# Two first value projections in one pass over x, and other banks, queues and orders of work at the seams

## The chip, the cores and the metric

The kernel runs on one core of one Trainium2 chip. The metric is the device time of one execution in microseconds. TensorE (PE) multiplies matrices, VectorE (DVE), ScalarE (ACT) and GpSimd (POOL) work on elements, SyncE (SP) issues most of the DMAs. Matmul results stand in PSUM banks, all other data in SBUF.

## What is computed

One transformer layer with native sparse attention (NSA) and a large feed-forward network, a gated embedding, and behind it a second layer with sliding-window attention (SWA) and a convolutional feed-forward network. There are 256 tokens with 2048 features, all in float32. Cut to what matters here:

```python
def first_block(x, ...):
    hn = rms_norm(x, norm_mix)
    q, kc, vc, ks, vs, kw, vw, gates = split(hn @ nsa_w_in)        # 16 heads of 128, 4 groups of keys
    k_cmp = silu(blocks(kc) @ w1_k) @ w2_k                          # and v_cmp: the compression
    o = g0 * att(q, k_cmp, v_cmp) + g1 * att(q, ks, vs) + g2 * att(q, kw, vw)
    h = x + o @ nsa_w_out
    h = h + square(relu(rms_norm(h, norm_ffn) @ ffn_w1)) @ ffn_w2
    h = h + (p @ ple_w_proj) * sigmoid(rms_norm(h, norm_ple) @ ple_w_gate)
    return rms_norm(h, norm_final)

def second_block(x, ...):
    q, k, v = split(rms_norm_2(x, g0) @ swa_w_in)                   # 32 heads of 64, 8 of keys
    x = x + rms_norm_2(softmax_with_sinks(q, k, bias) @ v @ swa_w_out, g1)
    return x + rms_norm_2(conv_ffn(rms_norm_2(x, g2)), g3)
```

## The kernel before, in words

**Numbers in two parts.** Every float32 operand is split into a high part that PE multiplies exactly and a low rest. ScalarE writes the high part (L264 for weights, L379 and L382 for activations), DVE the low one (L265, L380, L383). A product takes three matmuls: high by high, high by low, low by high (L350 to L352 with weights as the moving operand, L329 and L330 with weights as the stationary one).

**Weights** are one stream in the order of their use, in blocks of 128 x 128. A DMA brings 16 blocks (1 MB, L248) into one of three raw buffers; 8 blocks are a unit, which is split into one of four split buffers. `take` hands out blocks and has units split three ahead (`LOOK`).

**The beginning** (`build`, from L479). x comes as eight tiles of two blocks (128 features by 256 tokens each), between the first weights on SP's queue (`load`, L235). In a loop over the 16 blocks, each is split with its gain, its square is added to a sum on POOL (L395, L396), and it is multiplied into vs, the values of the selected attention. A unit of weights serves two blocks. `nsa` then multiplies all of x again into vw, the values of the window attention, and takes the mean square (L403).

**The first attention** (`nsa`, L559). Projections (32 matmuls each) of kc, vc, the gates, keys and queries follow each other in a list of steps. `compress` is a generator whose pieces are run between them: its last piece has a chain of PE, ScalarE and PE again (L844 to L849). Per pair of heads `scores` runs one step behind the queries, `flip` (transposes of p) two steps later and `values` one more. PSUM is two pools: two banks "mm" (`ps_mm`) for projections and six banks "att" (`ps_att`) for the rest. `scores` takes four of "att": three for scores (L655 to L657) and one for compressed scores (L662), which DVE reads at L690 after eight maxima (L683). `flip` takes four: three for p (copied at L379 and L380) and one for the compressed p (copied at L733). One step in six has both.

**The output projection** loads x again as residual (L804, SP's queue) when the attention's memory is free, adds it (L815), and transposes the sum (`columns`, L458).

**The second attention** (`swa`, L938) has 16 pairs of heads; the exponentials are at L1004, four parts a pair: the first two are one head's. POOL multiplies all four by the reciprocal of their sum (L1011, L1013), then PE transposes them (L1022 to L1024).

**The end of the second attention.** The output projection runs in four groups of 512 columns, each with two halves of tokens b. Each half is squared and summed on ScalarE (L412), multiplied by its gain on DVE (L1090, `evict`). Behind the last group one factor for both halves is worked out, eight residual steps follow (L1111), and `columns` transposes and splits the result for the convolutional network, whose first four tiles (`mm_beside`, L339 and L340) take each block as it comes. `mm_rows_last` (L354) is there already for the very end: it holds four split units and multiplies all that belongs to one half, then the other.

**Order.** Each engine has one queue in order. A planner lays the queues out at compile time from the order of the code, by when operands and buffers should be ready; `issue_after` puts instructions behind a named one on its engine.

Of the kernel before, what the change touches and what calls it, by code (L numbers as in the profile page):

```python
# [9 lines left out]
F32R = mybir.dt.float32r  # L10
AF = mybir.ActivationFunctionType
ALU = mybir.AluOpType

P = 128
# [98 lines left out]
def _stream(a):  # L113
# [4 lines left out]
    kv = {n: w[:, 2048 + 512 * i : 2560 + 512 * i] for i, n in enumerate(("kc", "vc", "ks", "vs", "kw", "vw"))}  # L118
    out.add(0, _g_major(kv["vs"]), _g_major(kv["vw"]))
    gates = np.zeros((KD, P, P), np.float32)  # L120
# [105 lines left out]
class Weights:  # L226
# [7 lines left out]

    def load(self, upto, between=None):  # L235
        while self.n_dma < min(upto, self.n):
            c = self.n_dma
            t = self.pool.tile([P, 16 * P], F32, tag="w_raw", name=f"w_raw{c}", bufs=W_RAW)
            half = UNIT * P
            if c < W_RAW:  # L240

                for n in range(2):
                    s = slice(n * half, (n + 1) * half)
                    between(2 * c + n)
                    for s in (slice(0, half // 2), slice(half // 2, half)) if c + n == 0 else (s,):
                        self.nc.sync.dma_start(t[:, s], self.src[c][:, s])
            else:
                self.nc.sync.dma_start(t, self.src[c])  # L248
            self.raw[c] = t
            self.n_dma += 1  # L250
# [42 lines left out]
class Program:  # L293
# [185 lines left out]
    def build(self):  # L479
# [22 lines left out]
        def load_x(i):  # L502
            nc.sync.dma_start(x0[i], ins["x"][:, 2 * i : 2 * i + 2])

        self.w.load(W_RAW, load_x)
        for i in range(2 * W_RAW, KD // 2):
            load_x(i)
        nc.scalar.dma_start(cst, ins["cst"])
# [11 lines left out]
        acc = self.tile(x_pool, [P, S], F32, "acc")  # L520
        self.ps_vs = [self.ps_att(), self.ps_att()]
        for k in range(KD):
            src = x0[k // 2][:, k % 2]
            if k % 2 == 0:
                self.w.split(k // 2 + 1)
            x = self.slot(k, F32R)
            self.split512(x, src, self.vec(V_MIX + k))
            self.add_square(acc, src, k == 0)
            xs.append(x)
            self.mm_rows(self.ps_vs, [x], k == 0, k == KD - 1)  # L530
        self.pad(self.base, 96)
# [27 lines left out]
    def nsa(self, xs, acc):  # L559
        tc, nc = self.tc, self.nc  # L560
        kv_pool = pool = tc.alloc_tile_pool(name="nsa", bufs=1)

        vhi, vlo, ps_v = {}, {}, {}
        for name in ("s", "w"):
            vhi[name] = self.tile(pool, [P, 2, 512], F32R, f"vhi_{name}")
            vlo[name] = self.tile(pool, [P, 2, 512], F32R, f"vlo_{name}")
            if name == "s":
                ps_v[name] = self.ps_vs
            else:
                ps_v[name] = [self.ps_att(), self.ps_att()]  # L570
                self.mm_rows(ps_v[name], xs)
        rc = self.rsqrt(self.mean_square(acc))
# [57 lines left out]
        for f, i in ((lambda r: key(0, r), 0), (lambda r: key(0, r), 1), (query, 0), (query, 1)):  # L630
            f(i)
            next(cv)
        self.pad(cpool, ALIGN - 32)
        cpool.release()
# [6 lines left out]

        sm, pt = {}, {}

        def scores(i):
# [4 lines left out]
            for h in range(2):  # L649
                q = qs[2 * i + h]  # L650
                for b in range(2):
# [5 lines left out]
                    nc.tensor.matmul(dst, lhsT=ql, rhs=k_h[:, :n], start=False, stop=True)  # L657
            psc = self.ps_att()
            for b in range(2):
# [51 lines left out]
        def flip(i):  # L711

            p0, p1 = sm.pop(i)
            banks = []
            for r in range(2):
                t = self.ps_att()
                for h in range(2):
                    nc.tensor.transpose(t[:, h * S : h * S + P], p0[:, h, r], self.ident)
                    nc.tensor.transpose(t[:, h * S + P : (h + 1) * S], p1[h][:, 0, r], self.ident)
                banks.append((t, P, 512))  # L720
            t = self.ps_att()
            for r in range(2):
                for h in range(2):
                    at = r * S + h * P
                    nc.tensor.transpose(t[:, at : at + P], p1[h][:, 1, r], self.ident)
            banks.append((t, P, 512))
            t = self.ps_att()
            for h in range(2):
                for b in range(2):
                    at = h * S + b * P  # L730
                    nc.tensor.transpose(t[:48, at : at + P], pc[:, 2 * b + h].bitcast(F32), self.ident)
            ct = self.tile(pool, [48, 512], F32R, "pth3")
            nc.scalar.activation(ct, t[:48], AF.Copy)  # L733
            out = []
            for n, (t, rows, cols) in enumerate(banks):
                hi = self.tile(pool, [rows, cols], F32R, f"pth{n}")
                lo = self.tile(pool, [rows, cols], F32R, f"ptl{n}")
                self.split(hi, lo, t[:rows, :cols])
                out.append((hi, lo))
            pt[i] = out + [ct]  # L740
# [50 lines left out]

        heads = [o[h // 2][:, h % 2] for h in range(16)]
        ps = [self.ps_mm(), self.ps_mm()]
        for h in range(0, 12, 3):
# [7 lines left out]
        for g in range(NG):  # L802
            for b in range(2):
                nc.sync.dma_start(self.hres[b][g], self.ins["xn"][:, b, g * COLS : (g + 1) * COLS])  # L804
        self.acc = self.tmp("racc", 2, (P, 2, NG))
# [14 lines left out]
    def compress(self, pool, name, raw, pos, kc, vc):  # L820
        nc = self.nc
        ps = self.ps_att()
        for c in range(4):
# [10 lines left out]
            for l in range(8):  # L834

                nc.tensor.matmul(ps[:, : 2 * P], lhsT=parts[:, l].rearrange("p a n -> p (a n)"),
                                 rhs=self.w.take_both(), start=c + l == 0, stop=c == 3 and l == 7)
            if c < 3:
                yield
        t = self.tile(pool, [P, P], F32, "cz")  # L840
# [4 lines left out]
        h = self.tile(pool, [P, G, 16], F32, f"ch_{name}")  # L845
        nc.scalar.activation(h.rearrange("p g n -> p (g n)"), ps[:, :64], AF.Silu)
        ps = self.ps_att()
        if name == "k":
# [89 lines left out]
    def swa(self):  # L938
# [33 lines left out]
        def scores(t):  # L972
# [39 lines left out]
            for c, _, dst, _ in parts:  # L1012
                nc.gpsimd.tensor_scalar(dst, dst, f[:, c : c + 1], 1.0, op0=ALU.mult, op1=ALU.mult)  # L1013
            sm[t] = p
# [76 lines left out]

        for g in range(NG):
            if g == 0:
# [6 lines left out]
            if g == NG - 2:  # L1100
                self.ready_sqrt(acc[:, 0, g : g + 1])
        r6 = self.rsqrt(*self.row_mean(acc))
        self.acc = self.tmp("racc", 2, (P, 2, NG))
        self.xs = []
        lows = []
        for g in range(NG):

            with tc.issue_after(lows[g - 2].ins) if g > 1 else contextlib.nullcontext():
                for b in range(2):
                    h = hres[b][g]  # L1110
                    step = nc.vector.scalar_tensor_tensor(h, ms[b][g], r6[:, b : b + 1], h, op0=ALU.mult, op1=ALU.add)  # L1111
            self.xs += self.columns([hres[b][g] for b in range(2)], g, 0, V_G2 + 32, alone=True)
            lows.append(self.last_low)
            if g == 0:
                self.first_step = step

# [130 lines left out]
```

## Time and profile before

| | |
|---|---|
| median of 3 runs | 2250.23 us (2249.52 to 2252.89) |
| the profiled execution | 2248.71 us, span 2246.9 us |
| granted clock of PE, mean share of 2.4 GHz | 0.995 |
| busy | PE 2213.7, DVE 1445.9, ACT 1180.3, POOL 247.8 us |
| moved by DMA | 415.64 MB, 185 GB/s over the span |

In the profile, busy is the time in which an engine worked on any instruction. A matmul's end is modelled, so short gaps between matmuls can hide in it; the time from one start to the next shows them. An idle time is put down to what ended it. "Released by" below means just that.

### The profile page before, as it was taken

The page shows a single profiled execution, that of the slowest core. Times are in us where ns is not written, and L with a number is a line of the kernel's source. Part 1 is how long each engine was busy: PE and PEld are TensorE (multiplying, and loading weights), DVE is VectorE, ACT ScalarE, POOL GpSimd, SP SyncE. Part 2 cuts the span into 40 slices and gives each one's busy share as a digit, 9 for nine tenths or more (in the row PEclk, how much of TensorE's full clock was granted, in tenths as well). Part 3 has the DMA queues.
Part 4 walks back from the last instruction along what each step waited for, and adds up shares of the span by engine and source line. Part 5 has one row for each costly group of instructions (what it writes and reads, how often), then busy time and mean ns, then how long its engine had stood idle before and what let it go on. Part 6 is the DMA issues. An engine that isn't in the chain of part 4 may idle for free. (4 is left out here: it accounts for less than half of the span.)

```text
span 2246.9 us, 29986 instructions
## 1 busy us (share of the span) xinstructions
PE 2213.7 (99%) x11645; PEld 1887.4 (84%) x11645; DVE 1445.9 (64%) x2181; ACT 1180.3 (53%) x1894; POOL 247.8 (11%) x309
## 2 busy tenths in 40 slices
PE   8999999999999999999999999999999999999998
PEld 6888887888888888888888888778888888888886
DVE  7676665666544566645566777557765765775775
ACT  4566554545433455544466566446555554554554
POOL 6431220000000000000000123102100100110110
PEclk9999999999999999999999999999999999999999
DMA  7553335565555555555555544444555555555553
GB/s 256 191 203 132 113 130 197 184 213 187 190 197 194 188 196 197 189 188 192 193 203 190 199 157 147 166 169 169 207 187 191 201 189 190 201 191 189 200 191 131
DMA packets 65951, 415.64 MB, mean 185 GB/s; under 512 B 7409, under 2 KB 12529, under 8 KB 17425
## 3 DMA queue, kind: packets, MB, share of 16 engines
q1 hardware_dynamic: 65376, 413.01, 51.8%
q8 instruction: 91, 1.49, 0.3%
q10 hardware_dynamic: 432, 0.73, 0.1%
q14 instruction: 52, 0.42, 0.1%
HBM read 410.03 MB, written 3.67 MB: 184 GB/s over the span
## 5 line engine op out<-in xcount | busy, mean ns | idle before, releaser
L265 DVE TENSOR_TENSOR w_split<-w_raw,w_split 128x1024 fp32r<-128x1024 f32 (+1 forms) x759 | 947.4, 1249 | 618.3 <-ACT w_split L264 612.4
L264 ACT ACTIVATE w_split<-w_raw 128x1024 fp32r<-128x1024 f32 (+1 forms) x759 | 801.9, 1057 | 674.4 <-PE att L352 447.6
L329 PE MATMUL mm<-slot,w_split 128*128 128x512 f32 x3152 | 1092.3, 393 | 1.3 <-DVE z L373 1.3
L330 PE MATMUL mm<-slot,w_split 128*128 128x256 f32 x3152 | 877.4, 278 | 0.0
L329 PEld LDWEIGHTS mm<-slot,w_split 128*128 128x128 f32 x3152 | 593.1, 188 | 131.6 <-issue 3.2
L330 PEld LDWEIGHTS mm<-slot,w_split 128*128 128x128 f32 x3152 | 595.1, 189 | 0.3
L351 PE MATMUL att<-w_split,h 128*128 128x512 f32 x848 | 330.3, 389 | 0.0
L352 PE MATMUL att<-w_split,h 128*128 128x512 f32 x848 | 330.1, 389 | 0.0
L350 PE MATMUL att<-w_split,h 128*128 128x512 f32 x848 | 330.0, 389 | 0.0
L371 ACT ACTIVATE t<-mm 128x256 f32<-128x256 f32 x201 | 76.2, 379 | 219.0 <-PE mm L330 217.7
L350 PEld LDWEIGHTS att<-w_split,h 128*128 128x128 f32 x848 | 159.2, 188 | 33.0
L352 PEld LDWEIGHTS att<-w_split,h 128*128 128x128 f32 x848 | 159.2, 188 | 32.9
L351 PEld LDWEIGHTS att<-w_split,h 128*128 128x128 f32 x848 | 159.2, 188 | 32.8
L1134 POOL TENSOR_TENSOR u<-z,rb 128x256 f32<-128x256 f32 x88 | 73.7, 838 | 673.7 <-DVE z L373 565.4
L373 DVE TENSOR_TENSOR z<-mm,t 128x256 f32<-128x256 f32 x201 | 84.3, 420 | 75.6 <-ACT t L371 75.3
L351 PE MATMUL att<-w_split,slot 128*128 128x512 f32 x320 | 125.9, 393 | 4.0 <-DVE w_split L265 3.9
L350 PE MATMUL att<-w_split,slot 128*128 128x512 f32 x320 | 125.3, 393 | 1.8 <-ACT w_split L264 1.8
L352 PE MATMUL att<-w_split,slot 128*128 128x512 f32 x320 | 125.8, 393 | 0.0
L946 POOL MEMSET vh<- 128x512 f32 x1 | 0.5, 527 | 901.9 <-DVE sum L418 901.9
L351 PEld LDWEIGHTS att<-w_split,slot 128*128 128x128 f32 x320 | 60.4, 189 | 19.2 <-DVE w_split L265 6.8
L350 PEld LDWEIGHTS att<-w_split,slot 128*128 128x128 f32 x320 | 60.2, 189 | 15.3 <-ACT w_split L264 3.0
L352 PEld LDWEIGHTS att<-w_split,slot 128*128 128x128 f32 x320 | 60.4, 189 | 12.5 <-DVE slot L383 0.5
(261 smaller groups left out, 1906.4 us busy)
## 6 DMA issues: line engine op xcount, KB each, us to landing
w_raw<-in_w SPq DMA_DIRECT2D x376, 1024.0 KB, 4.8
bias<-bandd SPq DMA_DIRECT2D x32, 128.0 KB, 2.7
w_raw<-in_w SPq DMA_DIRECT2D x5, 512.0 KB, 7.6
x<-in_x SPq DMA_DIRECT2D x8, 256.0 KB, 7.1
slot<-in_xn SPq DMA_DIRECT2D x8, 256.0 KB, 8.0
gain<-in_rows SPq DMA_DIRECT2D x2, 1024.0 KB, 6.6
out<-slot SPq DMA_DIRECT2D x8, 256.0 KB, 2.0
bandd<-rows SPq DMA_DIRECT2D x2, 768.0 KB, 6.6
```

The source lines that it names most:

```text
L264: nc.scalar.activation(hi[:, c], raw[:, c], AF.Copy)
L265: nc.vector.tensor_tensor(lo[:, c], raw[:, c], hi[:, c].bitcast(F32), op=ALU.subtract)
L329: nc.tensor.matmul(ps, lhsT=hi, rhs=x, start=i == 0, stop=False)
L330: nc.tensor.matmul(ps[:, S:], lhsT=lo, rhs=x[:, :S], start=False, stop=i == n - 1)
L350: nc.tensor.matmul(ps[b], lhsT=xh, rhs=hi, start=first and i == 0, stop=False)
L351: nc.tensor.matmul(ps[b], lhsT=xh, rhs=lo, start=False, stop=False)
L352: nc.tensor.matmul(ps[b], lhsT=xl, rhs=hi, start=False, stop=last and i == n - 1)
L371: nc.scalar.activation(t, ps[:, S : 2 * S], AF.Copy)
L373: nc.vector.tensor_tensor(z, ps[:, :S], t, op=ALU.add)
L946: nc.gpsimd.memset(t[:, :, :, 64:128].bitcast(F32), 0.0)
L1134: nc.gpsimd.tensor_tensor(u[:, 2:], self.total(ps), rb, op=ALU.mult)
```

## The change

It has six parts.

- The weights of vs and vw are interleaved block by block in the stream, one unit holding four blocks of each, and the loop over x multiplies every block into both, into four "att" banks. The second pass is gone. x comes as 16 transfers of one block: six between the first weights, the rest two ahead of each later weight transfer.
- `compress` yields after each of its four parts and once more behind the SiLU; the k chain is taken up in the loop over keys and queries, and the rest of the v chain is run out behind it.
- In `nsa` the compressed scores and the flip's fourth tile take a bank of "mm" until the output projection begins, and of "att" from there on.
- The first two residual tiles are loaded from ScalarE's queue.
- In `swa` ScalarE multiplies the first head's two parts of p, POOL the second's.
- The last group of the second attention's output uses `mm_rows_last`; each half has a factor of its own. The first half is evicted and stepped for all four groups, and its first eight blocks transposed into four banks, ahead of the second half's eviction in the code.

```diff
@@ _stream
-    out.add(0, _g_major(kv["vs"]), _g_major(kv["vw"]))
+    both = [_g_major(kv[n]).reshape(KD, 4, P, P) for n in ("vs", "vw")]
+    out.add(0, np.concatenate(both, axis=1).reshape(-1, P, P))
@@ load
             else:
+                if 2 * c < KD:
+                    for n in range(2):
+                        self.between(2 * c + n)
                 self.nc.sync.dma_start(t, self.src[c])
@@ build
-            nc.sync.dma_start(x0[i], ins["x"][:, 2 * i : 2 * i + 2])
+            nc.sync.dma_start(x0[i // 2][:, i % 2], ins["x"][:, i])
...
-            if k % 2 == 0:
-                self.w.split(k // 2 + 1)
+            self.w.split(k + 1)
...
-            self.mm_rows(self.ps_vs, [x], k == 0, k == KD - 1)
+            for ps in self.ps_v:
+                self.mm_rows(ps, [x], k == 0, k == KD - 1)
@@ nsa
-                self.mm_rows(ps_v[name], xs)
...
             next(cv)
+            next(ck, None)
+        for _ in cv:
+            pass
...
+        side = self.ps_mm
...
-            psc = self.ps_att()
+            psc = side()
...
-            t = self.ps_att()
+            t = side()
...
+        side = self.ps_att
         ps = [self.ps_mm(), self.ps_mm()]
...
-                nc.sync.dma_start(self.hres[b][g], self.ins["xn"][:, b, g * COLS : (g + 1) * COLS])
+                eng = nc.sync if g else nc.scalar
+                eng.dma_start(self.hres[b][g], self.ins["xn"][:, b, g * COLS : (g + 1) * COLS])
@@ compress
-            if c < 3:
-                yield
+            yield
...
         nc.scalar.activation(h.rearrange("p g n -> p (g n)"), ps[:, :64], AF.Silu)
+        yield
@@ swa, scores
-                nc.gpsimd.tensor_scalar(dst, dst, f[:, c : c + 1], 1.0, op0=ALU.mult, op1=ALU.mult)
+                if c < 2:
+                    nc.scalar.activation(dst, dst, AF.Copy, scale=f[:, c : c + 1])
+                else:
+                    nc.gpsimd.tensor_scalar(dst, dst, f[:, c : c + 1], 1.0, op0=ALU.mult, op1=ALU.mult)
@@ swa, the end
-        for g in range(NG):
+        for g in range(NG - 1):
...
-        r6 = self.rsqrt(*self.row_mean(acc))
+        def factor(b):
+            return self.rsqrt(*self.row_mean(acc[:, b : b + 1]))
+        def step(b, g):
+            h = hres[b][g]
+            return nc.vector.scalar_tensor_tensor(h, ms[b][g], r6[b], h, op0=ALU.mult, op1=ALU.add)
+        def turn(k, b):
+            nc.tensor.transpose(early[k // 2][:, k % 2 * S + b * P : k % 2 * S + (b + 1) * P],
+                                hres[b][k // 4][:, k % 4 * P : (k % 4 + 1) * P], self.ident)
+        ps = [self.ps_att(), self.ps_att()]
+        halves = self.mm_rows_last(ps, heads)
+        next(halves)
+        evict(NG - 1, 0, ps)
+        r6 = [factor(0)]
+        for g in range(NG):
+            step(0, g)
+        next(halves)
+        early = [self.ps_att() for _ in range(4)]
+        for k in range(8):
+            turn(k, 0)
+        evict(NG - 1, 1, ps)
+        r6.append(factor(1))
...
-                for b in range(2):
-                    h = hres[b][g]
-                    step = nc.vector.scalar_tensor_tensor(h, ms[b][g], r6[:, b : b + 1], h, op0=ALU.mult, op1=ALU.add)
-            self.xs += self.columns([hres[b][g] for b in range(2)], g, 0, V_G2 + 32, alone=True)
+                last = step(1, g)
+            if g < 2:
+                for k in range(4 * g, 4 * g + 4):
+                    turn(k, 1)
+                    x = self.slot(k, F32R)
+                    self.split512(x, early[k // 2][:, k % 2 * S : (k % 2 + 1) * S], self.vec(V_G2 + 32 + k))
+                    self.xs.append(x)
+            else:
+                self.xs += self.columns([hres[b][g] for b in range(2)], g, 0, V_G2 + 32, alone=True)
...
-                self.first_step = step
+                self.first_step = last
```

## Rows read from the trace of the kernel before

**Rows 1.** The page: busy us, share of the span and instructions of each engine

```profile
PE 2213.7 (99%) x11645; PEld 1887.4 (84%) x11645; DVE 1445.9 (64%) x2181; ACT 1180.3 (53%) x1894; POOL 247.8 (11%) x309
```

**Rows 2.** Waits of PE: line, releaser: us in total, times, longest

```profile
PE att L458 <- DVE slot L1111: 3.7, 1, 3.7
PE att L655 <- ACT pth L733: 3.6, 2, 1.8
PE att L1023 <- POOL p L1013: 2.4, 4, 1.2
...
PE mm L458 <- DVE slot L815: 1.7, 1, 1.7
...
PE att L849 <- ACT ch_k L846: 1.1, 1, 1.1
```

**Rows 3.** Windows: us, busy PE PEld DVE ACT POOL, granted clock, DMA, GB/s

```profile
33.00:59.00 26.00, 26.00 (x116) 21.49 (x115) 15.59 (x12) 9.55 (x9) 9.92 (x7) 1.00 0.64 223
...
270.00:276.50 6.50, 6.50 (x24) 5.73 (x24) 5.15 (x29) 3.76 (x17) 0.76 (x2) 0.50 0.17 71
...
1423.50:1427.00 3.50, 3.50 (x10) 2.82 (x11) 1.02 (x2) 0.87 (x2) 0.00 (x0) 0.51 0.53 222
...
1508.90:1515.70 6.80, 5.55 (x23) 5.18 (x24) 6.70 (x16) 3.14 (x8) 0.00 (x0) 0.50 0.01 2
```

**Rows 4.** Timeline (start, us, instruction), POOL's line by source, DMA of 5:20

```profile
4.75 0.62 POOL L395 TENSOR_TENSOR sq<-x 128x256 f32<-128x256 f32 x1
...
7.32 1.22 PE L350 MATMUL att<-w_split,slot 128*128 128x512 f32 x2 [1.63 <-ACT w_split L264]
...
12.46 1.63 DVE L265 TENSOR_TENSOR w_split<-w_raw,w_split 128x1024 fp32r<-128x1024 f32 x1
...
25.34 1.76 DVE L265 TENSOR_TENSOR w_split<-w_raw,w_split 128x1024 fp32r<-128x1024 f32 x1
...
59.02 0.50 PE L403 MATMUL att<-cst,acc 128*128 128x2 f32 x4
...
L395 POOL TENSOR_TENSOR sq<-x x7: 793/1590/1594, 12.2 to 24.3; 128x256 f32<-128x256 f32 x7
...
DMA packets 2244, 6.14 MB, mean 409 GB/s; under 512 B 256, under 2 KB 256, under 8 KB 2148
```

**Rows 5.** Timeline of the first attention, a step with a flip and scores

```profile
218.79 0.50 PE L655 MATMUL att<-kh,q 128*128 128x512 f32 x1 [1.82 <-ACT pth L733]
...
222.67 0.22 DVE L690 TENSOR_TENSOR sc<-att,cst 128x64 f32<-128x64 f32 x1
```

**Rows 6.** Second attention: exponentials (ns min/median/max), weight loads that waited, the last normalising

```profile
L1004 ACT ACTIVATE p<-p,top x64: 386/448/512, 1285.3 to 1418.3; 128x128 f32<-128x128 f32 x32, 128x256 f32<-128x256 f32 x32
...
  PEld att L1023: 6.7, 15
...
1419.61 3.70 POOL L1013 TENSOR_SCALAR p<-p,f 128x128 f32<-128x128 f32 x4 [5.34 <-DVE f L1011]
```

**Rows 7.** Timeline of DVE where the first residual is added

```profile
349.32 0.69 DVE L815 TENSOR_TENSOR slot<-mm,slot 128x512 f32<-128x512 f32 x1 [2.04 <-DMA slot<-in_xn]
```

**Rows 8.** Timeline of PE and DVE at the second attention's end

```profile
1506.01 0.39 PE L352 MATMUL att<-w_split,slot 128*128 128x512 f32 x1
...
1506.48 1.43 DVE L1090 TENSOR_TENSOR slot<-att,slot 128x512 f32<-128x512 f32 x2 [0.44 <-ACT junk L412]
...
1509.34 2.74 DVE L1111 SCALAR_TENSOR_TENSOR slot<-slot,rs_o,slot 128x512 f32<-128x512 f32 x4
...
1512.02 3.26 DVE L383 SCALAR_TENSOR_TENSOR slot<-att,vecs,slot 128x256 fp32r<-128x256 f32 x8
...
1513.05 0.78 PE L339 MATMUL mm<-slot,w_split 128*128 128x512 f32 x1
...
1532.27 1.23 DVE L265 TENSOR_TENSOR w_split<-w_raw,w_split 128x1024 fp32r<-128x1024 f32 x1 [0.58 <-ACT w_split L264]
...
1533.41 0.16 DVE L439 RECIPROCAL rs_r<-rs_y 128x2 f32<-128x2 f32 x1
```

More of the change, by code (lines that the diff above doesn't have):

```diff
@@ L235, in load @@
     def load(self, upto, between=None):
+        if between:
+            self.between = between
         while self.n_dma < min(upto, self.n):
@@ L242, in load @@
                 for n in range(2):
+                    self.between(2 * c + n)
                     s = slice(n * half, (n + 1) * half)
-                    between(2 * c + n)
                     for s in (slice(0, half // 2), slice(half // 2, half)) if c + n == 0 else (s,):
@@ L247, in load @@
             else:
+                if 2 * c < KD:
+                    for n in range(2):
+                        self.between(2 * c + n)
                 self.nc.sync.dma_start(t, self.src[c])
@@ L502, in load_x @@
         def load_x(i):
-            nc.sync.dma_start(x0[i], ins["x"][:, 2 * i : 2 * i + 2])
+            nc.sync.dma_start(x0[i // 2][:, i % 2], ins["x"][:, i])
         self.w.load(W_RAW, load_x)
-        for i in range(2 * W_RAW, KD // 2):
-            load_x(i)
         nc.scalar.dma_start(cst, ins["cst"])
@@ L520, in build @@
         acc = self.tile(x_pool, [P, S], F32, "acc")
-        self.ps_vs = [self.ps_att(), self.ps_att()]
+        self.ps_v = [[self.ps_att(), self.ps_att()] for _ in range(2)]
         for k in range(KD):
             src = x0[k // 2][:, k % 2]
-            if k % 2 == 0:
-                self.w.split(k // 2 + 1)
+            self.w.split(k + 1)
             x = self.slot(k, F32R)
@@ L561, in nsa @@
         kv_pool = pool = tc.alloc_tile_pool(name="nsa", bufs=1)
-        vhi, vlo, ps_v = {}, {}, {}
+        vhi, vlo = {}, {}
+        ps_v = dict(zip(("s", "w"), self.ps_v))
         for name in ("s", "w"):
@@ L566, in nsa @@
             vlo[name] = self.tile(pool, [P, 2, 512], F32R, f"vlo_{name}")
[L567 to L570, printed above, removed]
-                self.mm_rows(ps_v[name], xs)
         rc = self.rsqrt(self.mean_square(acc))
@@ L1101, in swa @@
                 self.ready_sqrt(acc[:, 0, g : g + 1])
-        r6 = self.rsqrt(*self.row_mean(acc))
+        def factor(b):
[19 more added lines that the diff above has]
+        r6.append(factor(1))
+        assert next(halves, None) is None
         self.acc = self.tmp("racc", 2, (P, 2, NG))
```

## The prediction

> **What bounds the kernel now.** I read the shares of busy time first: TensorE (PE) is busy for 2213.7 of 2246.9 us [rows 1], so nothing but PE's idle time and PE's slow time can be won. The change adds no matmul and takes none away. Next I read the list of PE's waits, longest in total first [rows 2]: each names a place where two stages meet, and all but the small ones lie at a place that the diff touches. Then the stretches with the granted clock [rows 3]: three times the clock fell from 2.4 to 1.2 GHz in the middle of the work, each time right behind one of those waits, and there PE counts as busy at half speed. That is hidden from the first view. A wait thus has two prices: itself, and now and then the slow time behind it. Not every wait has the second: of two waits of 1.8 us at L655, the first [rows 5] was followed by no drop, the second was.
>
> **Part A, the first pass over x.** Today 96 matmuls for vs follow x as it is split, and 96 for vw run as a second pass. In the second pass PE is full: 116 starts in 26.00 us, so 0.226 us a matmul [rows 3]. The first is uneven: PE starts at 7.32 us and both passes are over at 59.02 us [rows 4], 51.7 us for 192 x 0.226 = 43.4 us of work. The change does 12 matmuls (2.71 us) per block of x where it did 6, with one unit of weights for each block, not for two.
>
> What must keep up: VectorE (DVE) has one low split of weights and one of x per block. Beside POOL's squares a weight split took 1.63 to 1.76 us, and five of them, each with two splits of x, started 12.88 us apart from first to last, 3.22 us a round [rows 4]. With POOL idle a weight split takes 1.23 us and a split of x 3.26 / 8 = 0.41 us [rows 8]. So POOL's squares stretch 1.23 + 0.82 = 2.05 us to 3.22. For one split of each I take 1.65 + 0.75 = 2.4 us, under PE's 2.71. ScalarE needs less, and a block's 640 KB take 1.6 us at the 409 GB/s of the opening [rows 4]. PE becomes the limit as soon as the second unit is split. Today that is at 12.46 + 1.63 = 14.1 us; 256 KB less of x lie ahead of it (0.6 us), so 13.5 us, and what is left then is 11 + 14 x 12 = 179 matmuls, 40.5 us: the pass ends at 54.0 us, 5.0 us sooner. I take 4.5, since splits of x may again be queued ahead of the weights that are needed first. Bounds: 7.0 (PE never waits after 7 us; 43.4 us and 1.6 us for matmuls at the lower clock in the first 3 us) and 2.2 (rival 1). The eight more transfers of x (16 of 128 KB for 8 of 256) are issued by SP between waits of its own; those that now stand among the later weights are there long before block 6. POOL's sum of squares is needed right behind the pass; with 7 squares in the four rounds [rows 4], 16 blocks take 29 us from 4.8 us on, so it is done by some 35 us, and by 45 us if the denser work of DVE slows it by a third.
>
> By the Trainium skill (SBUF — State Buffer, section SBUF: two separate sides) a DVE instruction with two SBUF inputs and a GpSimd instruction that reads SBUF exclude each other for the whole instruction. The rows above show less than that: a round with 1.75 squares and sums on POOL, 2.2 us of it alone, is stretched by 1.2 us. By the rule the pass would go by rival 1.
>
> **Part B, the compression.** More yields put a projection between the links of the k chain. The 1.1 us wait at L849 [rows 2] goes; bounds 0 and 1.1, since nothing else waits for kc until the first scores.
>
> **Part C, the first attention (L655 to L733).** At a step with a flip and scores eight banks of the pool of six are wanted, so the second head's late scores wait until ScalarE has copied the flip's fourth bank: 1.82 us, twice [rows 2, 5]. The change draws two of the eight from the other pair, "mm": six and two fit. What is late next is that pair: the projection behind the scores needs a bank of it. One holds the flip's fourth tile until ScalarE's copy, which ends just ahead of 218.79 us, the other the compressed scores [rows 5]. Without the wait the last three score products start at 218.79 - 1.82 = 216.97 us and the projection is due no sooner than 217.65 (three of 0.226), so at most 1.1 us stay; eight small products lie between as well, so I take 0.3 at each of the two places: 3.0 us won. With the wait goes the drop behind the second one: 6.50 us at half the clock, 3.3 us [rows 3]. Sum 6.3, bounds 0 (the wait only moves) and 7.
>
> **Part D, the second attention.** Four POOL multiplies normalise p; the last head's take 3.70 us beside DVE's weight splits, and the transposes wait for them one by one [rows 6]. PE's idle time there is 2.4 us in the list [rows 2], but weight loads for the transposes waited 6.7 us in 15 places [rows 6]; a transpose that starts late delays all behind it, so the second is nearer to the price. ScalarE takes two of four at the 0.39 to 0.51 us of its exponentials on the same shapes [rows 6], beside POOL's two, so the last link comes at about half the time. Bounds 2.4 and 6.7; I take 5.5, since the first head and the last, where the step is shortest, will keep some. The drop behind the last head, 3.5 us at 0.51, goes with it: 1.7 us [rows 3]. What it costs: ScalarE gets some 0.9 us a head more and, in order, stands still until the reciprocal is there; the weight splits queued behind it are for units three ahead, 3 x 2.7 us off. Sum 7.2.
>
> **Part E, the end of the second attention.** Today the last group's two halves end together; 6.65 us after PE's last product (1506.01 and 0.39) the next stage's first matmul runs, at 1513.05 us [rows 8]. The change splits the last eight heads by half, so the first half's eviction, factor, four residual steps and eight transposes can lie beside or behind the other half's 24 matmuls (5.4 us). Behind the last product are then one residual step, not two, and one transpose. Best case: factor at 1509.34 as today, one step 0.69, transposes counted as one product 0.23, two splits 0.82, with some 0.1 between, so 1511.2: 1.85 us won, and the 1.3 us that the low clock cost between 1513.05 and 1515.7 [rows 3]. But DVE has it all to do in that time: eviction 0.72, the chain to the factor 1.43 (1507.91 to 1509.34), four steps 2.74 [rows 8], and three weight splits of 1.23 us, whose buffers now come free only in the second half. That is 8.6 us from 0.7 us into a 5.4 us stretch: the second half's eviction, behind it in DVE's queue, starts 3.9 us after the last product where it could at 0.7. Small chains do get pushed back so: a weight split at 1532.27 us made the reciprocal behind a ready root wait until 1533.41 [rows 8]. Worst case: 3.2 - 1.0 = 2.2 us lost and up to 1.8 us more at the low clock. I take a loss of 1.5, nearer to the worse end, because the weight splits are older in the code than all they push back; bounds +3.1 and -4.0.
>
> **Part F, the residual.** The first residual waits for x rows queued behind a 1 MB weight transfer on SP [rows 7]; PE lost 1.7 us [rows 2]. From ScalarE's queue it shares the engines with that transfer and is in time. ScalarE's two issues fall into time when it has nothing to do. I take 1.7; bounds 0 and 1.7.
>
> **Sum.** 4.5 + 1.1 + 6.3 + 7.2 + 1.7 - 1.5 = 19.3 us. The profiled execution took 2248.71 us (span 2246.9 and 1.8 around it): 2229.4 us. The median of the runs shown is 1.5 us above the profiled one, so 2231 us.
>
> **Rivals.** (1) DVE and POOL pace the first pass: 1.23 + 0.41 us and two POOL instructions of 0.62 us [rows 4, 8] one after the other are 2.88 us a block against 2.71. Fifteen blocks lose 2.3 us more: A brings 2.2, the time is 2233. The stretched rounds above speak against it; chance 0.15. (2) One attention stage keeps its waits, C because "mm" takes their place or D because ScalarE comes no earlier than POOL did: 2237 to 2244 us. ScalarE's order of work, which no row of before shows, decides; 0.22. (3) Slower: the pair "mm" becomes the bound of the first attention. A projection that finds both held must wait as the scores do today. If all ten steps that draw on the pair paid 1.82 us, that is 18 us, with a drop of 3.3 us behind every second one 35, and C's 6.3 not won: 2231 + 41 = 2272. It decides as soon as both banks are held when a projection starts. Against it: the compressed scores are read 4 us after L655's last group starts [rows 5], and a projection (16 products of 512 columns and 16 of half as many) takes 5.4 us; 0.05. (4) The gains are eaten up elsewhere, E at its worst and other orders of work: within 0.2%; 0.07. (5) All goes well, E too: 2216 to 2222; 0.06.
>
> **How the numbers follow.** Forecast 2231 us (2222 to 2237 for its own case), 0.45. Faster by over 0.2% (4.5 us, about what a measurement of this kernel can tell from no change) are the forecast, (1), (2) and (5): 0.45 + 0.15 + 0.22 + 0.06 = 0.88. Same 0.07, slower 0.05. All bounds together give 2221 to 2250; the range of 8 in 10 leaves out (3), most of (4) and the better half of (5): 2220 to 2244.
>
> **What would show it.** Right: 192 matmuls of L350 to L352 over by 54 us; no wait at L655 or L849, none of L1022 to L1024 for POOL but at the first and the last head; the clock full from about 10 us to the end of the second attention; L815 without a DMA as releaser. Wrong: PE's first products waiting for w_split all through the pass (1); L329 waiting for DVE L690 or ScalarE L733 (3); L1022 waiting for ScalarE (2); residual steps and weight splits between the last product and the second factor (E). The prediction falls if the sum of PE's waits does not shrink by some 10 us.

## The result, and the profile after

The changed kernel takes 2239.29 us (median of five runs, 2236.52 to 2241.78), the kernel before in the same session 2250.23 (2249.27 to 2253.44): ratio 0.9947, 95% interval 0.9933 to 0.9962. That is 10.9 us faster; 19.3 were forecast. The profiled execution took 2241.22 us (span 2239.4). The same kernel was profiled twice more, in another session, at 2234.03 and 2237.96 us, and that turns out to matter.

The first two views answer [rows 1] and [rows 2]: PE's share of busy time is what it was, and the list of its waits has other lines. The waits at L655, L849 and, but for two small ones, at the second attention's flips are gone; new ones stand at the fold of the compression (L850, the matmul that reads cz), ahead of it for a split of weights (L336), and at the turns of part E (L1121: the early transposes), and the residual's (L464) has grown. The page's waits, those over 0.15 us, sum to 22.1 us before and to 16.3, 16.9 and 18.0 in the three profiles of the changed kernel.

```profile
PE 2213.1 (99%) x11645; PEld 1890.3 (84%) x11645; DVE 1443.2 (64%) x2188; ACT 1190.8 (53%) x1927; POOL 228.6 (10%) x277
```

```profile
PE att L1121 <- DVE slot L1118: 4.3, 2, 2.5
PE mm L464 <- DVE slot L822: 2.2, 2, 1.7
PE att L850 <- DVE cz L848: 1.9, 1, 1.9
...
PE att L1121 <- DVE slot L389: 0.8, 1, 0.8
PE att L1033 <- POOL p L1023: 0.8, 2, 0.5
PE mm L336 <- DVE w_split L271: 0.8, 1, 0.8
PE mm L335 <- ACT pth L738: 0.7, 2, 0.3
```

Windows with the granted clock (columns as in [rows 3]). The low clock has moved with the waits: from behind L655 and the last flip to behind the fold of the compression and the residual; behind the second attention's end it holds for 10.2 us where it held for 6.8.

```profile
33.00:54.00 21.00, 21.00 (x94) 17.38 (x93) 17.42 (x15) 9.65 (x12) 11.13 (x11) 1.00 0.64 225
143.40:146.70 3.30, 3.30 (x13) 2.38 (x12) 2.04 (x3) 1.31 (x2) 0.00 (x0) 0.50 0.42 129
264.00:271.00 7.00, 6.67 (x38) 5.81 (x39) 5.39 (x26) 5.92 (x22) 0.00 (x0) 1.00 0.35 144
341.40:344.70 3.30, 3.30 (x11) 2.63 (x10) 2.21 (x5) 2.15 (x6) 0.00 (x0) 0.50 0.71 245
1408.00:1412.00 4.00, 3.64 (x18) 2.44 (x18) 2.46 (x4) 3.70 (x9) 1.87 (x2) 1.00 0.26 33
1495.10:1505.20 10.10, 7.49 (x29) 5.94 (x30) 8.69 (x21) 3.29 (x8) 0.00 (x0) 0.50 0.40 155
```

The places that answer [rows 4], [rows 5] and [rows 6] (timeline of PE; groups of operations of the second attention): the shared pass is over at 54.12 us, PE waits 0.33 us for the flip's copy, and ScalarE does half of the normalising.

```profile
54.12 0.50 PE L409 MATMUL att<-cst,acc 128*128 128x2 f32 x4
...
216.10 0.50 PE L335 MATMUL mm<-slot,w_split 128*128 128x512 f32 x1 [0.33 <-ACT pth L738]
...
L1023 POOL TENSOR_SCALAR p<-p,f 128x256 f32<-128x256 f32 x15 | 16.5, 1102 | 0.0
...
L1021 ACT ACTIVATE p<-p,f 128x256 f32<-128x256 f32 x15 | 7.4, 494 | 0.0
```

Cutting the span where PE starts certain products shows where the time went (us, start to start, read from the timelines):

| stretch, up to | part | before | changed | second profile | third profile |
|---|---|---|---|---|---|
| first compression matmul | A | 94.45 | 89.31 | 89.39 | 90.31 |
| first scores, first attention | B | 56.48 | 59.40 | 58.17 | 59.44 |
| last values, first attention | C | 189.15 | 182.38 | 181.97 | 182.55 |
| first matmul of the first feed-forward into an "mm" bank | F | 80.69 | 82.79 | 80.75 | 80.87 |
| last matmul of the second projection | D | 1085.24 | 1078.19 | 1078.02 | 1078.14 |
| 128th matmul of the up product | E | 32.20 | 35.46 | 34.83 | 35.81 |
| first matmul of the down product | - | 111.32 | 114.17 | 111.34 | 111.32 |
| end of the span | - | 597.39 | 597.74 | 597.75 | 597.74 |

In the first profile A, C and D won 5.1, 6.8 and 7.0 us, B lost 2.9, E 3.3 and F 2.1 (next to nothing in the other two), and 2.85 went in a stretch of plain matmuls that no part touches. No run undoes A, C or D alone; what each is worth is read from its stretch.

### The profile page after: what moved, and what is told of

It reads as the page before. It is cut to its first block, busy times and chain, and to the rows that moved or that the text cites. A ratio compares the mean times of both kernels' runs of the same rounds, so it can differ in the third digit from the quotient of the medians.

```text
span 2239.4 us, 30016 instructions
## 1 busy us (share of the span) xinstructions
PE 2213.1 (99%) x11645; PEld 1890.3 (84%) x11645; DVE 1443.2 (64%) x2188; ACT 1190.8 (53%) x1927; POOL 228.6 (10%) x277
## 4 chain that ended last, share of the span: by engine, by line
PE 94%; DVE 2%; ACT 2%; POOL 1%; issue 1%; DMA 1%; DVEq 0%; SPq 0%; POOLq 0%; ACTq 0%
PE mm L335 31%; PE mm L336 15%; PE att L356 13%; PE att L357 13%; PE att L358 13%; DVE w_split L271 1%; PE mm L345 1%; PE att L345 1%; ACT w_split L270 1%; PE mm L464 1%; PE mm L356 0%; PE mm L357 0%; PE mm L358 0%; PE mm L346 0%; DMA slot<-in_xn 0%
## 5 line engine op out<-in xcount | busy, mean ns | idle before, releaser
L336 PE MATMUL mm<-slot,w_split 128*128 128x256 f32 x3152 | 878.2, 279 | 0.8 <-DVE w_split L271 0.8
L336 PEld LDWEIGHTS mm<-slot,w_split 128*128 128x128 f32 x3152 | 595.0, 189 | 1.4 <-DVE w_split L271 1.1
L356 PE MATMUL att<-w_split,slot 128*128 128x512 f32 x304 | 119.9, 396 | 1.6 <-ACT w_split L270 1.6
L358 PE MATMUL att<-w_split,slot 128*128 128x512 f32 x304 | 119.9, 394 | 0.0
L357 PE MATMUL att<-w_split,slot 128*128 128x512 f32 x304 | 119.4, 393 | 0.0
L356 PEld LDWEIGHTS att<-w_split,slot 128*128 128x128 f32 x304 | 57.8, 190 | 14.6 <-ACT w_split L270 3.0
L357 PEld LDWEIGHTS att<-w_split,slot 128*128 128x128 f32 x304 | 57.8, 190 | 11.9
L358 PEld LDWEIGHTS att<-w_split,slot 128*128 128x128 f32 x304 | 57.7, 190 | 12.0
```

The source lines that it names most:

```text
L336: nc.tensor.matmul(ps[:, S:], lhsT=lo, rhs=x[:, :S], start=False, stop=i == n - 1)
L356: nc.tensor.matmul(ps[b], lhsT=xh, rhs=hi, start=first and i == 0, stop=False)
L357: nc.tensor.matmul(ps[b], lhsT=xh, rhs=lo, start=False, stop=False)
L358: nc.tensor.matmul(ps[b], lhsT=xl, rhs=hi, start=False, stop=last and i == n - 1)
```

## The experiments

All are variants of the changed kernel unless said otherwise; the kernel before stood at 2250.6 to 2251.2 us beside them.

**The end as before (E undone).**

```
-        halves = self.mm_rows_last(ps, heads)
...
+        r6 = self.rsqrt(*self.row_mean(acc))
```

> The changed kernel with the end of the second attention put back as it was before (both halves of the last bank evicted together, one factor, no early turns); the other five parts stay. In the profiles this stretch, from the last matmul of the output projection to the first matmul of the first down product, took 143.5 us before and 149.6 us after. Theory: the halves themselves cost this, so the stretch goes back to 143.5 and the time falls by about 6, from 2239.3 to some 2233. Rival, the size of the forecast: the halves cost 1.5 us and the rest (matmul pairs of the first up product at 349 ns where they took 340 before) is nothing of theirs, so the stretch stays at 148 and the time at 2237 to 2238.

2235.27 us (ratio 0.9934, 0.9922 to 0.9947). Up to the 128th matmul 32.16 us where the changed kernel has 35.46, and the plain stretch behind it 111.31. Of the 6.1 us between the two profiles 3.3 are E's; the other 2.85 left too, in plain matmuls that ran at another pace, of which two later runs say more. Between the medians it is 4.0 us.

**The compression's steps as before (B undone).**

```
-            next(ck, None)
-        for _ in cv:
-            pass
...
-            yield
+            if c < 3:
+                yield
```

> The changed kernel with the compression's steps put back (three yields, the value chain inside the loop); the other five parts stay. From the first compression matmul to the first score matmul the profiles show 56.5 us before and 59.4 after. Theory: B itself turned its 1.1 us gain into a 2.9 us loss, since the value chain lost its cover (PE waits 1.88 us for cz at 140.5 and runs at the lower clock for 3.4 us behind it): with B undone the wait of 1.1 for ch_k comes back, the 1.88 and the clock drop go, the stretch is 56.5 and the time about 2236.5. Rival: the wait for cz comes from where the weight splits stand since the pass through x is shared (part A), and stays: the stretch is 59 to 60.5 and the time 2239 to 2240.5.

2237.10 us (0.9942, 0.9929 to 0.9954). The stretch takes 56.47 us, as before: the wait for ch_k is back at 1.1 and that for cz is 0.07. The theory's number holds. Its picture, a value chain without cover, does not: PE's order around the fold is the same in both. What differs is below, first the changed kernel, then the one with B undone (timelines; z is the projected query before POOL multiplies it by rb).

```profile
136.82 2.36 DVE L271 TENSOR_TENSOR w_split<-w_raw,w_split 128x1024 fp32r<-128x1024 f32 x2 [0.52 <-ACT w_split L270]
137.64 0.36 ACT L377 ACTIVATE t<-mm 128x256 f32<-128x256 f32 x1
...
139.09 0.42 DVE L379 TENSOR_TENSOR z<-mm,t 128x256 f32<-128x256 f32 x1
139.43 1.22 DVE L271 TENSOR_TENSOR w_split<-w_raw,w_split 128x1024 fp32r<-128x1024 f32 x1
139.59 1.63 POOL L599 TENSOR_TENSOR qf<-z,rb 128x256 f32<-128x256 f32 x1 [4.21 <-DVE z L379]
...
141.58 0.26 ACT L847 ACTIVATE cz<-att 128x128 f32<-128x128 f32 x1
...
142.38 0.32 PE L850 MATMUL att<-cst,cz 128*128 128x64 f32 x1 [1.88 <-DVE cz L848]
```

```profile
137.88 0.42 DVE L379 TENSOR_TENSOR z<-mm,t 128x256 f32<-128x256 f32 x1 [0.89 <-ACT t L377]
...
138.38 0.73 POOL L599 TENSOR_TENSOR qf<-z,rb 128x256 f32<-128x256 f32 x1 [5.82 <-DVE z L379]
...
138.83 1.37 DVE L271 TENSOR_TENSOR w_split<-w_raw,w_split 128x1024 fp32r<-128x1024 f32 x1 [0.52 <-ACT w_split L270]
```

With B, z is late twice. Its last input is there at 138.00 us, but two weight splits hold DVE until 139.09. Then a third split is ready, DVE takes it, and POOL's product of the query needs 1.63 us beside it where it needs 0.73 alone. ScalarE's copies, cz among them, queue in order behind that product. B also costs PE two waits for split weights, 0.8 and 0.3 us near 125 us; with B undone both are gone.

**The first keys' and queries' product on DVE.**

```
-            nc.gpsimd.tensor_tensor(out, z, rb, op=ALU.mult)
+            eng.tensor_tensor(out, z, rb, op=ALU.mult)
...
+            self.split512(qs[h], project(qf[h], nc.gpsimd if h > 1 else nc.vector))
```

> The changed kernel with one difference: the multiplication by rb of the first two keys and two queries (128x256) is on DVE, where it was on POOL. In the changed kernel POOL needs 1.63 to 1.65 us for it while DVE splits a weight unit, and 0.74 where DVE is idle. Theory: the wait of 1.88 us for cz at 140.5 is made by that: z behind a weight split on DVE, POOL held up by the next split, ACT's q and cz in order behind it. With the multiplication on DVE the wait falls under 0.6 and the clock drop behind it goes, from the first compression matmul to the first scores it takes 55.3 to 56.5 us instead of 59.4, time 2235 to 2236.5. Rival: the value chain lacks cover in PE's order, whatever POOL does: the wait stays at 1.3 or more, 58.5 to 59.5, time 2238.5 to 2240.

2234.49 us (0.9927, 0.9913 to 0.9940). The stretch takes 54.51 us, 4.9 less than in the changed kernel and 2.0 less than before, with no wait of PE left in it: better than the theory said, since B's own gain of 1.1 us is now kept. The planner also laid DVE's queue out anew: z starts at 136.03 us, as soon as its input is there, and only then come the product and the split. So this run takes away both delays at once, z behind two splits and POOL beside the third, and does not tell how much each was worth.

**The residual's transfers all on SP (F undone).**

```
-                eng = nc.sync if g else nc.scalar
-                eng.dma_start(self.hres[b][g], ...
+                nc.sync.dma_start(self.hres[b][g], ...
```

> The changed kernel with all eight residual transfers on SP again; the other five parts stay. Theory: they land when the DMA engines have moved the 1 MB of weights issued just ahead of them, whichever queue issues them, so PE's waits ahead of the first transposes behind the first attention stay at 2.2 us in all (0.52 and 1.67), the median landing at 8 us, and the time within 0.5 us of 2239.3. Rival, the forecast's step: the other queue brings the first two 1.25 us earlier, so without it the waits grow to 3.4 us and the time to 2240.5 or more.

2236.70 us (0.9944, 0.9932 to 0.9957). One wait of 1.6 us instead of 0.5 and 1.7, landing after 7.7 us as a median, stretch 80.38 us. The queue does not matter for the landing. The time is 2.6 us below what the theory said, but the changed kernel's own five runs lie 5.3 us apart, so the whole times do not tell the two kernels apart.

**The residual ahead of the weights.**

```
+        with tc.issue_after(xn.ins):
+            self.w.load(self.w.n_split // 2 + W_RAW)
```

> The changed kernel with one difference: the weight transfers of 1 MB whose turn would come while the last heads of the first attention are projected are queued on SP behind the six residual transfers. Theory: the residual is late because of the bytes ahead of it on the DMA engines, not because of a queue: 1 MB less ahead of 2 MB lets the first land 2 us earlier or more, PE's waits ahead of the transposes (2.2 us) fall to 0.5 or less and no lower clock follows; time 2235.5 to 2237 unless the weights are then late. Rival: what sets them is SP's issue (0.89 us each, six in a row), so that the later four land as now and the wait of 1.67 stays: 2239.

2237.75 us (0.9938, 0.9926 to 0.9950), above the theory's 2237; its profile has the slower pace of plain matmuls (342 in 60 us). The waits are gone, as the theory said, and the stretch falls to 78.70 us, 2 less than before. DVE's additions, changed kernel first, then this one:

```profile
337.47 0.69 DVE L822 TENSOR_TENSOR slot<-mm,slot 128x512 f32<-128x512 f32 x1 [0.54 <-DMA slot<-in_xn]
...
339.94 0.69 DVE L822 TENSOR_TENSOR slot<-mm,slot 128x512 f32<-128x512 f32 x1 [1.78 <-DMA slot<-in_xn]
```

```profile
338.30 1.28 DVE L828 TENSOR_TENSOR slot<-mm,slot 128x512 f32<-128x512 f32 x2
```

The bytes ahead were the cause. The Trainium skill (DMA: Bandwidth & Descriptors, section Issuing engines are not separate DMA queues) says that DMAs of several engines run on the same 16 DMA engines and that spreading them saves issue time alone. These runs agree: 7.7 us to the landing on one queue, 6.8 and 8.0 on two, 4.5 and 5.7 with 1 MB less ahead.

**E with the weight splits held back.**

```
+        self.w.look = 0
         w = [self.w.take(4) for _ in range(n)]
+        self.w.look = LOOK
...
+                with tc.issue_after(last.ins):
+                    self.w.split(self.w.at // UNIT + LOOK)
```

> The changed kernel with one difference: the weight splits whose buffers come free during the second half of the last bank are queued behind the first step of the second half's rows, where now three of them (1.23 us each on DVE, 1.06 on ACT) stand among the seven small operations of the first half's factor. Theory: they are what makes the first half's turns late, so PE's wait of 2.49 us ahead of them goes, the waits of this stretch fall from 5.1 us to 1 to 2.5, the lower clock from 10.2 us to 3.4 to 6.8, and the time by 3 to 5.5, to 2234 to 2236.5. Rival: the second half's own chain (eviction, factor, step) sets the end and the wait moves there, the waits sum to 4.5 or more and the time stays at 2238.5 to 2240.

2239.29 us (0.9947, 0.9933 to 0.9960): time and waits as the rival said, though this profile too has a slower pace of plain matmuls (341 in 60 us). The first up product starts 3.5 us earlier against the projection's end, but PE's waits still sum to 5.0, in five places, since the held splits now stand ahead of the columns' low parts:

```profile
PE att L1124 <- DVE slot L1121: 1.8, 1, 1.8
PE att L1124 <- DVE slot L392: 1.6, 2, 1.1
PE att L467 <- DVE slot L392: 0.9, 1, 0.9
PE att L467 <- DVE sum L427: 0.6, 1, 0.6
```

**E with the low parts of these splits on POOL.**

```
+        self.w.low = nc.gpsimd
         w = [self.w.take(4) for _ in range(n)]
+        self.w.low = nc.vector
```

> The changed kernel with one difference: the low parts of the weight units that are split while the last bank of the second attention is taken in two halves are formed on POOL instead of DVE (some six units of 1.2 us on DVE). Theory: the stretch between the output projection and the first up product is bound by DVE's whole work (eight steps of 0.69, sixteen low parts of 0.4 to 0.5, weight splits of 1.23, two factors), so that with three to four splits less on DVE it gets 2.5 to 4 us shorter: from the last matmul of the projection to the 128th of the up product 32 us instead of 35.5, waits and halved clock together. Rival: POOL beside DVE slows DVE's operations by as much as it takes over, or the weights come late from POOL, and the stretch stays at 35 or gets longer, with waits for w_split on PE.

2242.45 us (0.9956, 0.9944 to 0.9969), 38.2 us for the stretch, longer by 2.7, as the rival said. The timeline of POOL and DVE says why:

```profile
1487.64 7.04 POOL L272 TENSOR_TENSOR w_split<-w_raw,w_split 128x1024 fp32r<-128x1024 f32 x3 [4.41 <-ACT w_split L271]
...
1487.97 2.10 DVE L450 TENSOR_TENSOR rs_a<-rs_r 128x1 f32<-128x1 f32 x1
1490.11 2.29 DVE L451 TENSOR_TENSOR rs_a<-rs_a,ms 128x1 f32<-128x1 f32 x1
1492.43 0.15 DVE L452 TENSOR_SCALAR rs_a<-rs_a 128x1 f32<-128x1 f32 x1
1492.62 2.07 DVE L454 TENSOR_TENSOR rs_o<-rs_r,rs_a 128x1 f32<-128x1 f32 x1
```

Operations on one element per partition, 0.15 to 0.16 us alone, take over 2 us each, as long as a split on POOL (7.04 / 3 = 2.35 us). Only the one with a single tensor input runs freely.

**A, C and D alone**, put on the kernel before (B, E and F undone together).

> The kernel before with parts A, C and D alone: B (compression), E (halves) and F (residual's queue) are as before. Theory, from the runs so far: B costs the changed kernel 2.9 us, E 2.7 to 4, F nothing, so without them the time is 2232 to 2234, below both kernels, with the last matmul of the second attention's output projection 18 to 19 us earlier than before (A 4.9, C 6.8, D 7.0). Rival: what B and E cost is taken up elsewhere when they go together, since the time is set by the weights behind them: 2235 to 2237.

2230.35 us (0.9908, 0.9894 to 0.9922), better than forecast by the theory. Three parts carry the whole gain; B and E work against it, and F brings nothing.

**All three mended: E undone, the product on DVE, the residual first.**

> The changed kernel with three things put right: the end of the second attention as it was before, the multiplication by rb of the first two keys and queries on DVE instead of POOL, and the weight transfers of 1 MB behind the residual's. Theory: the three act in different stretches and add up, 4 us and 4.8 us and some 2 us less than the changed kernel's 2239.3, so 2227 to 2230, with no wait over 0.4 us on PE between 20 us and the end of the second attention but for the two of 0.33 ahead of pth. Rival: they don't add up, since each lowers the same lost clock or a later wait takes over: 2231 to 2234.

2227.45 us (0.9900, 0.9885 to 0.9915), the fastest of all and 11.8 us below the changed kernel. The gains add up.

**The same with E kept and DVE's order mended.**

```
+            with tc.issue_after(self.last_low.ins):
+                self.w.split(self.w.n_split + 1)
```

> The same as the kernel above, but with the two halves kept at the end of the second attention and DVE's order there changed: no weight split between the first half's eviction and the eighth low part of the turned columns, then one split after each four low parts. Theory: part E fails by DVE's order alone, so here the first half's turns run under the second half's matmuls, PE waits 2 to 3 us for the second half's factor and nothing later, and from the last matmul of the projection to the 128th of the up product it takes 31.5 to 32.5 us, where the changed kernel takes 35.5 and the end as before 32.2: 2226.5 to 2230, within a microsecond of the kernel above. Rival: DVE's whole work in the stretch is the bound, whatever its order: 34 us or more, 2230 to 2232.

2228.50 us (0.9903, 0.9886 to 0.9919). The total is near the theory's, the stretch is not: 34.9 us. Windows from the projection's last matmul to the 128th of the up product, in the kernel before, the changed one, the three mended, and this one (columns as in [rows 3]):

```profile
1506.00:1538.20 32.20, 28.45 (x161) 25.18 (x160) 25.44 (x52) 21.54 (x49) 0.00 (x0) 0.89 0.35 122
```

```profile
1492.10:1527.50 35.40, 30.30 (x161) 25.66 (x160) 26.44 (x55) 21.68 (x48) 0.00 (x0) 0.86 0.37 135
```

```profile
1483.20:1514.80 31.60, 27.85 (x161) 23.71 (x160) 25.33 (x51) 21.50 (x49) 0.00 (x0) 0.95 0.36 127
```

```profile
1483.20:1518.10 34.90, 31.09 (x161) 25.42 (x160) 26.70 (x51) 21.35 (x48) 0.00 (x0) 0.85 0.38 136
```

The same 161 matmuls. In the last kernel PE idles 34.90 - 31.09 = 3.8 us, no more than in the third (3.75), but is busy 3.2 us longer, at a mean clock of 0.85 where the third has 0.95. DVE's whole work is not the bound there, with 26.70 of 34.90 us busy. In the changed kernel idle time grew by 1.35 us over before and busy time by 1.85. So E cuts one wait into several, and much of PE's work between them runs at the lower clock. In the ten profiles with E the low clock behind the projection held for 6.8 to 13.7 us, in the four without for 3.4 to 6.8. That several waits keep it low is what these counts suggest; no run varied the number of waits alone. Nor does the length of the low clock alone set the stretch: with F undone it held for 6.8 us, as in the kernel before, and the stretch took 34.95 us; with E undone it held for 3.4 us, and the stretch took 32.16, as before (32.20).

**The changed kernel, unchanged, twice.**

> The changed kernel once more, unchanged, to see what of its profile belongs to the execution. Between 1560 and 1620 us its first profile holds 345 matmuls of the first up product, the kernel before and three variants 355, another variant 341, at the full granted clock in each. Theory: this pace belongs to the execution, not to the code, and is some 3 us of the time: where the profile holds 355 the time is 2236 to 2238, where it holds 341 to 345 it is 2239 to 2242. Rival: it belongs to the changed kernel's end of the second attention: 345 again with a time near 2237.

> The same kernel a third time, with the same two expectations: 355 matmuls between 1560 and 1620 us and 2236 to 2238 us of time, or 341 to 345 and 2239 to 2242, if the pace belongs to the execution; 345 with any time, if it belongs to the code.

2234.03 and 2237.96 us. Windows of equal length in the up product, changed kernel first, then its second profile:

```profile
1560.00:1620.00 60.00, 60.00 (x345) 52.71 (x343) 45.37 (x67) 34.38 (x55) 8.11 (x11) 1.00 0.53 191
```

```profile
1560.00:1620.00 60.00, 60.00 (x355) 53.26 (x354) 46.64 (x70) 36.11 (x57) 9.96 (x11) 1.00 0.56 200
```

345 matmuls against 355, with the full clock and no wait in both; the third profile has 355 too. One kernel shows both paces, so the code alone does not set it, and the variants of one session show both as well (355 with E undone and with F undone, 345 with B undone). Whether it goes by the execution or by something that differs between sessions stays open: the two later profiles are from one session and agree. It costs 114.17 - 111.34 = 2.8 us, the 2.85 in the table. The times given with it in the expectation were too narrow (2234.03 lay below them), because other things differ between profiles as well. Behind the wait at the fold the clock fell in the first and third profile (1.88 and 1.92 us) and not in the second (1.80); at the residual it fell behind the first profile's 1.67 us and not behind the 1.28 and 1.42 us of the others, nor behind 1.70 us in the kernel before.

## Why the prediction was right and wrong

The median, 2239.29 us, lies in the wide range (2220 to 2244), but above the forecast's own case (2222 to 2237). It lies where rival (2) put it, and not by rival (2)'s mechanism: neither attention stage kept its waits. By its own last sign the prediction falls, since the waits shrank by 4 to 6 us and not by some 10. Three parts came as worked out and three did not.

- **A**, forecast 4.5 us, measured 4.9 at the end of the pass (59.02 to 54.12); 5.1 and 3.9 in the other two profiles. PE ran at full pace from 13.7 us on, where the working had 13.5, but not for the working's reason: it did not wait for the second unit. Its matmuls started 0.43 us apart until then, as they did in the other two profiles at a granted clock of 0.50, up to 12.7 and 14.7 us. So the agreement in this term is in part luck. The window at 33 us shows the pace of the second pass before (94 matmuls in 21.00 us, then 116 in 26.00). DVE's weight splits began at 13.88, 16.32 and 18.75 us, 2.4 us a block as the working took it; rival (1) with 2.88 did not come. (Its price of 2.3 us should have been 2.6, fifteen times 0.17.)
- **C**, forecast 6.3, measured 6.8. The 0.3 us left at each of the two places is there (0.33). That the "mm" pair does not become the bound held too. Whether the 3.3 us of low clock in it belong to the kernel before or to its one profiled execution stays open, as the drops differ between profiles of one kernel.
- **D**, forecast 7.2, measured 7.0. From the first flip to the last it took 128.32 us instead of 133.88, 5.6 less with no low clock in either, where 5.5 were forecast. So the weight loads' wait of 6.7 us was nearer to the price than the 2.4 in PE's list.
- **B**, forecast a gain of 1.1, measured a loss of 2.9, 1.7 and 3.0 in the three profiles. The step that failed is "nothing else waits": it looked for readers of kc and not at what the moved k chain does to the order of the weight splits. The wait of 1.1 us did go, but the one at the fold, 0.07 before, became 1.8 to 1.9, and some 1 us of waits for split weights came ahead of it.
- **F**, forecast 1.7, measured nothing (2.1 lost with a drop of the clock, 0.1 and 0.2 without). "Is in time" failed: the working itself said that the transfer shares the engines, and gave it no time for that.
- **E**, forecast a loss of 1.5, measured 2.6 to 3.6 in three profiles. The mechanism was right: three weight splits stand among the first half's small operations (timeline of DVE; then PE), and the half's first turn starts at 1494.95 us, not under the second half's products. The mis-sized term is the loss of 1.5 taken between the bounds: in the three profiles PE idles 1.3 to 2.0 us longer in the stretch than before (2.2 at worst in the working) and is busy 1.3 to 1.9 us longer (up to 1.8 there), so both came near the worst. But with DVE's order mended the loss stayed: PE idles no longer than before and is busy 31.09 - 28.45 = 2.6 us longer. So the splits were not the only cause, and what the rest is stays open.

```profile
1489.51 1.23 DVE L271 TENSOR_TENSOR w_split<-w_raw,w_split 128x1024 fp32r<-128x1024 f32 x1 [0.79 <-ACT w_split L270]
...
1490.93 1.23 DVE L271 TENSOR_TENSOR w_split<-w_raw,w_split 128x1024 fp32r<-128x1024 f32 x1
...
1492.34 1.23 DVE L271 TENSOR_TENSOR w_split<-w_raw,w_split 128x1024 fp32r<-128x1024 f32 x1
1493.48 0.15 DVE L451 TENSOR_TENSOR rs_o<-rs_r,rs_a 128x1 f32<-128x1 f32 x1
1493.56 0.68 DVE L1100 TENSOR_TENSOR slot<-att,slot 128x512 f32<-128x512 f32 x1
1494.15 2.73 DVE L1118 SCALAR_TENSOR_TENSOR slot<-slot,rs_o,slot 128x512 f32<-128x512 f32 x4
...
1494.95 1.94 PE L1121 MATMUL att<-cst,slot 128*128 128x128 f32 x8 [2.49 <-DVE slot L1118]
```

The median lay inside the wide range because A, C and D, 18.0 of the 19.3 us, came as worked out. The miss of 8 us is mostly B, F and E: against the forecast they fell short by 9.6, 5.7 and 8.1 us together in the three profiles (B 2.8 to 4.1, F 1.8 to 3.8, E 1.1 to 2.1). The rest is within what the runs of one kernel differ by.

## What to carry to other kernels

Price a moved step by what it does to the in-order queues it leaves and enters, not only by its readers: a chain moved between projections shifted weight splits so that a neighbour's input came late and its POOL product took twice as long. Count the bytes ahead of a late transfer before giving it another queue. Before a change of a few tenths of a per cent is explained from one profile each, profile one kernel twice: here two profiles of one kernel, from two sessions, differed by 7 us.

## What was not expected of the hardware

- One and the same stream of matmuls ran at two paces at the full granted clock, 355 and 345 in 60 us, in two profiles of one kernel; two variants showed 341 and 342. The pace could change at a wait of 1.3 us and then held to the end of the stretch (with E undone, from 350 to 340 ns for two matmuls). What sets it stays open.
- DVE and POOL held each other up for about as long as the other's whole instruction: beside POOL's splits 0.16 us became 2.1 to 2.3, and POOL's 0.73 became 1.63 beside a split on DVE. The prediction had read the stretched rounds of the first pass as less than that. The Trainium skill (SBUF — State Buffer, sections Who interferes with whom and SBUF: two separate sides) says that a DVE instruction with two SBUF inputs and a GpSimd instruction that reads SBUF contend, that the first to issue keeps the ports for the whole instruction, and that one with at most one such input, outside the two-port modes, does not contend. The five rows with the splits on POOL agree with each of these, the 0.15 us of L452 included.
